# Rows instead of token blocks: a rotary projection whose halves change places by DMA

## The chip, the cores and the metric

The program runs on one core of a Trainium2 chip. A core has five engines that run their own instruction streams and wait for each other through semaphores: TensorE (PE: matmuls and transposes, results in PSUM), VectorE (DVE), ScalarE (ACT), GpSimd (POOL) and SyncE (SP), which here issues every DMA. The metric is the device time of one execution in microseconds: the median of three runs before is 1894.84 us (1893.67 to 1897.88).

## The reference

Two transformer blocks on 512 tokens of width 1024. The first has two layers. Each normalises x, projects it with one wide matrix, runs four attentions (a: latent, b: sliding window of 128 tokens, c: top-128 keys chosen by an indexer, d: with forget gates), four heads of 64 each, adds their projection to x, and then an MLP of width 4096. The second block has three dilated window attentions, a pooling branch and gates. What the change touches is the rotary embedding of b and c:

```
x1, x2 = xf[..., :half], xf[..., half:]
out = concatenate([x1 * cos - x2 * sin, x2 * cos + x1 * sin])
q_b = rope(b_q.reshape(B, S, H, Dh), pos)      # 4 heads of 64
k_b = rope(b_k.reshape(B, S, 2, Dh), pos)      # 2 heads of 64, each serves two query heads
q_c = rope(c_q.reshape(B, S, H, Dh), pos)
k_c = rope(c_k.reshape(B, S, H, Dh), pos)
```

## The kernel before

All arithmetic is float32. A matrix product is made of three matmuls in a reduced 32-bit format (`mm3`, lines 160 to 162): every operand is held as a high part and a low part, and high x high, high x low and low x high are added in PSUM. `split` (lines 167 and 168) makes such a pair: ScalarE writes the high part, VectorE subtracts it from the source and writes the low part.

Weights come in chunks of at most 128 x 1024 numbers. SP fetches them into two raw buffers (`send`, line 124); ScalarE makes the high half (line 143), VectorE or POOL the low half (line 144); four such pairs are kept, two chunks ahead of use. SP's queue is in order, so a fetch that waits for a buffer holds everything behind it.

The normalised input is kept as hT: 8 tiles of 128 features x 512 tokens. There are two ways to project. `token_proj` takes 128 tokens as the stationary operand and 256 weight columns as the moving one: 8 x 3 matmuls for each of four token blocks, result tokens x features. `feature_proj` takes 128 weight columns as the stationary operand and all 512 tokens as the moving one: result features x tokens, in one PSUM bank.

The attention scores need queries and keys as features x tokens ("seg", four planes of 128 features: two heads each). `roped` (line 586) projects by token blocks: for each block, VectorE multiplies by the cosines (line 286) and the exchanged halves by the signed sines (lines 287 and 288), POOL adds (line 289), TensorE turns the block with two 128x128 transposes (line 606), and `split` writes it into seg. It is called four times in each layer: queries and keys of b (line 750 and the one behind it; the keys' projection carries the values too) and queries and keys of c (lines 827 and 828). `lagged` puts a block's turn behind the next block's projection.

The order on each engine is made at build time: the program is written attention by attention (ORDER: latent inputs, indexer, scores and top-k for three token blocks, a, d's projections, d, c, b, and four output projections), and a scheduler lists the instructions of each engine by priority and by when it believes their inputs are there. So the projections of c and b fill TensorE while attention d runs, whose softmax and the top-k search (lines 581 and 582) keep VectorE. On the chip every engine then keeps its list strictly in order.

Two pools of scratch tiles matter: "tmp" (1024 columns, three buffers: norm rows, MLP activations and others) and "t2" (512 columns, four buffers: `half`, line 105). The constants are loaded at the start on SP's queue by `consts_first` (line 490), behind x and the first two weight chunks and ahead of the third and fourth.

Of the kernel before, what the change touches and what calls it, by code (L numbers as in the profile page):

```python
# [11 lines left out]
F32 = mybir.dt.float32  # L12
F32R = mybir.dt.float32r
AF = mybir.ActivationFunctionType
ALU = mybir.AluOpType
# [3 lines left out]
P = 128  # L19
S = 512  # L20
NB = S // P
D = 1024
KD = D // P
# [9 lines left out]
AHEAD, RAWS, HIS, TMPS, HALVES = 2, 2, 4, 3, 4  # L33
# [21 lines left out]
def halves(ap):  # L55
    return ap[:, :HALF], ap[:, HALF:]


class Kern:
# [43 lines left out]
        return self.tmp.tile([P, D], F32, tag="tmp", name=self.name("tmp"), bufs=TMPS)  # L103

    def half(self):
        return self.tmp.tile([P, S], F32, tag="t2", name=self.name("t2"), bufs=HALVES)

    def stat(self, cols=16):
        return self.small.tile([P, 16], F32, tag="st", name=self.name("st"), bufs=11)[:, :cols]
# [375 lines left out]
    def consts_first(self):  # L485
        nc, c, t = self.nc, self.fc, self.t

        def load(name, shape, src):
            o = c.tile(shape, F32, tag=name, name=name)
            nc.sync.dma_start(o, src)  # L490
            return o

        self.rope64 = load("rope64", [P, NB, 128], t["c_rope64"].rearrange("(b p) c -> p b c", p=P))
        self.rope32 = load("rope32", [P, NB, 64], t["c_rope32"].rearrange("(b p) c -> p b c", p=P))
        self.causal = load("causal", [P, S], t["c_causal"])
        self.swa = load("swa", [P, 256], t["c_swa"])
        self.tri = load("tri", [P, P], t["c_tri"])
        self.full_spans = [(0, (i + 1) * P, self.causal[:, S - (i + 1) * P :]) for i in range(NB)]
        self.ones = c.tile([P, P], F32, tag="ones", name="ones")
        nc.vector.memset(self.ones, 1.0)  # L500
# [85 lines left out]
    def roped(self, hT, ch, sg, at, take=None):  # L586


        nc = self.nc
        step = 2 if take else 1  # L590

        def rotate(b):
            pj = self.token_proj(hT, ch, b, 256)
            r = self.half()[:, :256]
            rv = r.rearrange("p (h c) -> p h c", c=64)
            n = 256 // step
            self.rope(rv[:, ::step], pj[:, :n].rearrange("p (h c) -> p h c", c=64), self.rope64, b)
            if take:
                nc.gpsimd.tensor_copy(rv[:, 1::2], rv[:, ::2])
                take(b, pj[:, n:256])  # L600
            return r

        def turn(b, r):
            pt = self.psum("tq")[:, :256]
            for c in range(2):
                nc.tensor.transpose(pt[:, c * P : (c + 1) * P], r[:, c * P : (c + 1) * P], self.ident)
            o = [t[:, at : at + 2, b * P : (b + 1) * P] for t in sg]
            self.split(o[0], o[1], pt.rearrange("p (m c) -> p m c", m=2))

        self.lagged(rotate, turn)  # L610

    def layer(self, l, hT, block):
        mixed = {}
# [125 lines left out]
    def window(self, l, hT):  # L739
        nc, t = self.nc, self.t  # L740
        sink = self.att.tile([P, 4], F32, tag="sink", name=self.name("sink"), bufs=1)
        nc.sync.dma_start(sink, t["swa_sinks"][l].partition_broadcast(P))
        sg = self.seg()
        vs = [self.new_v() for _ in range(2)]

        def values(b, src):
            for g in range(2):
                self.put_v(vs[g], b, src[:, g * 64 : g * 64 + 64].unsqueeze(1).to_broadcast([P, 2, 64]))

        self.roped(hT, self.weights(2), sg, 0)  # L750
        self.roped(hT, self.weights(2), sg, 2, values)
        spans = [(max(0, i - 1) * P, P if i == 0 else 2 * P, self.swa[:, 128:] if i == 0 else self.swa)
                 for i in range(NB)]
        return self.two_pairs(
            sg, vs, BAND, spans=spans, scale=0.125, sink=lambda h: sink[:, h : h + 1]
        )
# [67 lines left out]

    def selected(self, l, hT):
        sg = self.seg()
        self.roped(hT, self.weights(2), sg, 0)
        self.roped(hT, self.weights(2), sg, 2)
        ch = self.weights(2)
        vs = [self.new_v() for _ in range(2)]  # L830
        for b in range(NB):
            pj = self.token_proj(hT, ch, b, 256)
            for n in range(2):
                self.put_v(vs[n], b, pj[:, n * P : (n + 1) * P].rearrange("p (h c) -> p h c", c=64))
        return self.two_pairs(sg, vs, FULL, spans=[(0, n, a) for a, n in self.dsa], scale=0.125)
# [272 lines left out]
    def pair_inputs(self, hp, hT):  # L1108

        nc = self.nc  # L1110
# [10 lines left out]
        for g, which in HEADS2:  # L1121
# [12 lines left out]
            if which < 2:  # L1134
                o = self.new_qk()
                self.split(nat(o[:, 0]), nat(o[:, 1]), perm(pj), 0.125 if which == 0 else None)
                qk[g, which] = o
                continue
            vT = self.half()
            nc.scalar.copy(nat(vT), perm(pj))  # L1140
            v = self.new_v()
            pt = self.psum("tq")
# [299 lines left out]
    return np.ascontiguousarray(np.concatenate([c, c, -s, s], axis=1))  # L1442


def _bucket(n):
    exact = 16
    nf = np.maximum(n, 1).astype(np.float32)
    large = exact + (
        np.log(nf / np.float32(exact)) / np.float32(math.log(2048 / exact)) * np.float32(16)
    ).astype(np.int32)  # L1450
    return np.where(n < exact, n, np.minimum(large, 31))


def _constants():
# [14 lines left out]
    for g, w in enumerate((2, 4, 8, 16)):  # L1469
        short[g, :w] = np.float32(w) / np.arange(1, w + 1, dtype=np.float32)  # L1470
    return {
        "c_rope64": _rope_table(64), "c_rope32": _rope_table(32), "c_causal": causal, "c_swa": swa,
        "c_tri": tri, "c_buckets": buckets, "c_short": short,
    }

# [27 lines left out]
```

## Time and profile before

| | |
|---|---|
| median of three runs | 1894.84 us |
| the profiled execution | 1898.58 us |
| its span, first to last instruction | 1896.6 us |
| TensorE busy | 1816.0 us (96%) |
| VectorE busy | 1097.8 us (58%) |
| ScalarE busy | 876.0 us (46%) |
| POOL busy | 565.1 us (30%) |
| mean granted TensorE clock | 0.983 of full speed |

The profile is one execution. Matmuls are pipelined and their ends are modelled: one that is shown for 0.28 us can be followed by the next after 0.12 us. So what a matmul costs is read from the distance of starts in the timeline, not from its duration. A wait is put down to the engine that ended it.

### The profile page before, as it was taken

To read this page: it belongs to the slowest core of one execution; us is meant where nothing else is said; L and a number is where in the kernel's file an instruction comes from. 1 tells how busy PE (TensorE), PEld (TensorE's weight loads), DVE (VectorE), ACT (ScalarE), POOL (GpSimd) and SP (SyncE) were. 2 spreads that over 40 slices of the span, in tenths; PEclk is the share of its full clock that TensorE was granted. 3 is DMA by queue.
4 is the path that set the end of the run, shared out by engine and by line. 5 is a ranking of instruction groups with operands and counts; after the bars stand their busy time and mean duration, and the time that the engine had idled before them with its cause. 6 is when DMAs were issued, how large, how long until landed. Compare 5 with 4: busy or idle time off the path is not lost.

```text
span 1896.6 us, 25797 instructions
## 1 busy us (share of the span) xinstructions
PE 1816.0 (96%) x9414; PEld 1523.1 (80%) x9414; DVE 1097.8 (58%) x2437; ACT 876.0 (46%) x1882; POOL 565.1 (30%) x396
## 2 busy tenths in 40 slices
PE   7899998999999998999989999999799999998998
PEld 7788876888877887988778888888687888787886
DVE  6899667555554457997674433433726535446444
ACT  5666765233322346567762232332435444545443
POOL 1334331111111104334321111111146544433454
PEclk9999999999999999999999999999899999999999
DMA  4222112444456322322132333333332332322242
GB/s 162 59 75 71 46 49 81 118 149 145 145 150 179 106 56 66 81 59 73 45 99 68 98 103 100 95 95 100 101 101 60 112 91 79 90 62 62 83 150 100
DMA packets 220652, 178.52 MB, mean 94 GB/s; under 512 B 14734, under 2 KB 191278, under 8 KB 220526
## 3 DMA queue, kind: packets, MB, share of 16 engines
q1 hardware_dynamic: 220526, 176.88, 31.7%
q8 instruction: 74, 1.21, 0.3%
q14 instruction: 52, 0.43, 0.1%
HBM read 172.50 MB, written 8.03 MB: 95 GB/s over the span
## 4 chain that ended last, share of the span: by engine, by line
PE 80%; DVE 10%; DMA 4%; ACT 3%; issue 2%; SPq 0%; POOL 0%; ACTq 0%; DVEq 0%; POOLq 0%
PE acc L160 20%; PE acc L161 20%; PE acc L162 20%; PE sc L160 5%; PE sc L161 4%; PE sc L162 4%; DMA raw<-in_w_in_dram 2%; PE tp L385 2%; PE pv L311 1%; PE pv L310 1%; DVE dsa L582 1%; DVE dsa L561 1%; DVE m L581 1%; DMA raw<-in_w_down_dram 1%; DVE wlo L144 1%
## 5 line engine op out<-in xcount | busy, mean ns | idle before, releaser
L143 ACT ACTIVATE whi<-raw 128x1024 fp32r<-128x1024 f32 (+6 forms) x288 | 289.4, 1005 | 630.7 <-PE acc L161 274.0
L160 PE MATMUL acc<-hTh,whi 128*128 128x512 f32 (+1 forms) x1128 | 437.1, 389 | 12.4 <-DVE wd L1225 5.7
L161 PE MATMUL acc<-hTl,whi 128*128 128x512 f32 (+1 forms) x1128 | 434.2, 385 | 0.9 <-DVE hTl L168 0.9
L162 PE MATMUL acc<-hTh,wlo 128*128 128x512 f32 (+1 forms) x1128 | 432.9, 384 | 0.0
L144 POOL TENSOR_TENSOR wlo<-raw,whi 128x1024 fp32r<-128x1024 f32 (+4 forms) x143 | 312.1, 2187 | 353.5 <-ACT whi L143 331.5
L144 DVE TENSOR_TENSOR wlo<-raw,whi 128x1024 fp32r<-128x1024 f32 (+2 forms) x145 | 176.1, 1215 | 195.6 <-ACT whi L143 192.8
L876 POOL TENSOR_TENSOR tmp<-tmp 128x512 f32<-128x512 f32 x64 | 104.4, 1633 | 609.9 <-ACT tmp L874 609.9
L160 PEld LDWEIGHTS acc<-hTh,whi 128*128 128x128 f32 x1128 | 214.4, 191 | 56.9 <-ACT ms L1222 5.9
L161 PEld LDWEIGHTS acc<-hTl,whi 128*128 128x128 f32 x1128 | 214.6, 190 | 41.4 <-DVE hTl L168 2.4
L162 PEld LDWEIGHTS acc<-hTh,wlo 128*128 128x128 f32 x1128 | 214.3, 190 | 39.9
L160 PE MATMUL acc<-whi,hTh 128*128 128x256 f32 (+3 forms) x512 | 158.7, 312 | 6.4 <-DVE v L168 4.3
L162 PE MATMUL acc<-whi,hTl 128*128 128x256 f32 (+3 forms) x512 | 157.0, 307 | 0.2
L161 PE MATMUL acc<-wlo,hTh 128*128 128x256 f32 (+3 forms) x512 | 155.7, 305 | 0.4 <-DVE wlo L144 0.4
L160 PEld LDWEIGHTS acc<-whi,hTh 128*128 128x128 f32 x512 | 100.2, 196 | 12.0 <-DVE v L168 4.8
L162 PEld LDWEIGHTS acc<-whi,hTl 128*128 128x128 f32 x512 | 100.1, 195 | 3.3 <-DVE hTl L168 1.1
L161 PEld LDWEIGHTS acc<-wlo,hTh 128*128 128x128 f32 x512 | 100.3, 196 | 2.8 <-DVE wlo L144 0.8
L160 PE MATMUL acc<-whi,act 128*128 128x512 f32 x256 | 99.0, 392 | 3.5 <-DVE x L894 3.5
L161 PE MATMUL acc<-wlo,act 128*128 128x512 f32 x256 | 100.1, 391 | 0.0
L162 PE MATMUL sc<-whi,act 128*128 128x512 f32 x256 | 99.6, 389 | 0.0
L161 PE MATMUL sc<-wlo,act 128*128 128x512 f32 x256 | 99.6, 389 | 0.0
L160 PE MATMUL sc<-whi,act 128*128 128x512 f32 x256 | 99.6, 389 | 0.0
L162 PE MATMUL acc<-whi,act 128*128 128x512 f32 x256 | 98.8, 391 | 0.1
(341 smaller groups left out, 3475.9 us busy)
## 6 DMA issues: line engine op xcount, KB each, us to landing
raw<-in_w_in_dram SPq DMA_DIRECT2D x92, 512.0 KB, 4.0
raw<-in_w_up_dram SPq DMA_DIRECT2D x64, 512.0 KB, 4.2
raw<-in_w_down_dram SPq DMA_DIRECT2D x64, 512.0 KB, 3.3
raw<-in_w_out_dram SPq DMA_DIRECT2D x24, 512.0 KB, 3.5
raw<-in_w_ada_dram SPq DMA_DIRECT2D x24, 512.0 KB, 4.0
raw<-in_w_in_dram SPq DMA_DIRECT2D x8, 416.0 KB, 5.3
x<-in_x_dram SPq DMA_DIRECT2D x4, 512.0 KB
nrow<-neg SPq DMA_DIRECT2D x8, 256.0 KB
```

Of the source, the lines that this page charges most:

```text
L143: self.nc.scalar.activation(hi, raw, AF.Copy)
L144: self.lo_engine.tensor_tensor(lo, raw, f(hi), ALU.subtract)
L160: mm(out, lhsT[0], rhs[0], start=first, stop=False)
L161: mm(out, lhsT[0], rhs[1], start=False, stop=False)
L162: mm(out, lhsT[1], rhs[0], start=False, stop=last)
L310: mm(out, both, th[0], start=first, stop=False)
L311: mm(out[0:64], v[:, j, x, 0], th[1], start=False, stop=False)
L385: nc.tensor.transpose(pt[:, at : at + P], hd["p"][:, src : src + P], self.ident)
L561: nc.vector.scalar_tensor_tensor(a, e, r[:, 288 + h : 289 + h], self.causal[:, S - n :] if h == 0 else a, ALU.mult, ALU.add)
L581: nc.vector.max(out=m8, in_=a)
L582: nc.vector.match_replace(out=a, in_to_replace=m8, in_values=a, imm_value=TAKEN)
L876: nc.gpsimd.tensor_tensor(r[:, S:], r[:, :S], r[:, :S], ALU.mult)
```

## The change

A new method, `roped_rows`, replaces `roped` for the queries of b and for the queries and keys of c; the keys of b stay with `roped`. It projects 128 features over all 512 tokens at once (two halves m of 24 matmuls each), copies the result to SBUF on ScalarE, and lets four DMAs on SP's queue write each group of 32 partitions to its partner's place in a second tile. VectorE multiplies both tiles by rows of a new constant table (ropeT: cosines and signed sines as features x tokens), POOL adds them, and `split` writes seg; no transpose is needed. The scratch tile `a, t` is one "tmp" tile of two halves. To make room, "t2" tiles shrink from 512 to 384 columns, and the value copies of the second block move from "t2" to "tmp".

```diff
     def half(self):
-        return self.tmp.tile([P, S], F32, tag="t2", name=self.name("t2"), bufs=HALVES)
+        return self.tmp.tile([P, 384], F32, tag="t2", name=self.name("t2"), bufs=HALVES)
...
         self.rope32 = load("rope32", [P, NB, 64], t["c_rope32"].rearrange("(b p) c -> p b c", p=P))
+        self.ropeT = load("ropeT", [P, 2, S], t["c_ropeT"].rearrange("n p c -> p n c"))
...
+    def roped_rows(self, hT, chunks, sg, at):
+
+        nc = self.nc
+        for m in range(2):
+            out, cs, n = self.psum("acc"), slice(m * P, (m + 1) * P), 0
+            for c in chunks:
+                for k in range(c[0].shape[1]):
+                    self.mm3(
+                        out, (c[0][:, k, cs], c[1][:, k, cs]), (hT[0][:, n], hT[1][:, n]), n == 0, n == KD - 1
+                    )
+                    n += 1
+            a, t = halves(self.scratch())
+            nc.scalar.copy(a, out)
+            for q in range(4):
+
+                o = q ^ 1
+                nc.sync.dma_start(t[o * 32 : o * 32 + 32], a[q * 32 : q * 32 + 32])
+            nc.vector.tensor_tensor(a, a, self.ropeT[:, 0], ALU.mult)
+            nc.vector.tensor_tensor(t, t, self.ropeT[:, 1], ALU.mult)
+            nc.gpsimd.tensor_tensor(a, a, t, ALU.add)
+            self.split(sg[0][:, at + m], sg[1][:, at + m], a)
...
-        self.roped(hT, self.weights(2), sg, 0)
+        self.roped_rows(hT, self.weights(2), sg, 0)
         self.roped(hT, self.weights(2), sg, 2, values)
...
     def selected(self, l, hT):
         sg = self.seg()
-        self.roped(hT, self.weights(2), sg, 0)
-        self.roped(hT, self.weights(2), sg, 2)
+        self.roped_rows(hT, self.weights(2), sg, 0)
+        self.roped_rows(hT, self.weights(2), sg, 2)
...
-            vT = self.half()
+            vT = self.scratch()[:, :S]
```

TensorE, queries of attention c in the first layer, before: `acc_2203` is the third token block's result, `tq_2198` the turned first block, `tp_1463` a softmax tile of attention d.

```order
L162 MATMUL acc_2203<-whi_1736,hTl_111 128x256
L385 MATMUL tp_1463<-ident,p_1426 128x128
L606 MATMUL tq_2198<-ident,t_476_2161 128x128 x2
L160 MATMUL acc_2203<-whi_1736,hTh_110 128x256
L161 MATMUL acc_2203<-wlo_1737,hTh_110 128x256
L162 MATMUL acc_2203<-whi_1736,hTl_111 128x256
L385 MATMUL tp_1463<-ident,p_1426 128x128
```

The same engine and projection after the change: `acc_2138` ends the first half of the features, `acc_2174` begins the second, and `tp_1403` is again a softmax tile of d.

```order
L162 MATMUL acc_2138<-hTh_112,wlo_1772 128x512
L160 MATMUL acc_2174<-hTh_112,whi_1738 128x512
L161 MATMUL acc_2174<-hTl_113,whi_1738 128x512
L162 MATMUL acc_2174<-hTh_112,wlo_1739 128x512
L160 MATMUL acc_2174<-hTh_112,whi_1738 128x512
L161 MATMUL acc_2174<-hTl_113,whi_1738 128x512
L162 MATMUL acc_2174<-hTh_112,wlo_1739 128x512
L160 MATMUL acc_2174<-hTh_112,whi_1738 128x512
L160 MATMUL sc_1444<-seg_1236 128x384
L161 MATMUL sc_1444<-seg_1237,seg_1236 128x384
L162 MATMUL sc_1444<-seg_1236,seg_1237 128x384
```

The narrow matmuls and the two transposes are gone; scores and value products of d stand between the wide ones, and the transposes into `tp_1403` follow 16 rows behind the last row of `acc_2138`. On TensorE 8589 rows remain of 8910.

VectorE, the first rotation of the same projection, before:

```order
L168 TENSOR_TENSOR pt_1406<-tp_1401,pt_1406 128x512
L582 MATCH_REPLACE dsa_491<-m_204_915,dsa_491 128x512
L286 TENSOR_TENSOR t_476_2161<-acc_2136,rope_98 128x256
L287 TENSOR_TENSOR t_477_2162<-acc_2136,rope_98 128x4x32
L288 TENSOR_TENSOR t_477_2162<-acc_2136,rope_98 128x4x32
L359 RECIPROCAL sa_1430<-sa_1428 128x4
```

And after the change, where `tmp_2163` is the scratch tile that the four DMAs fill:

```order
L407 TENSOR_TENSOR total_1231<-pv_1200,total_1231 64x512
L349 TENSOR_SCALAR sa_1431<-sa_1429 128x4
L168 TENSOR_TENSOR pt_1408<-tp_1403,pt_1408 128x512
L630 TENSOR_TENSOR tmp_2163<-tmp_2163,ropeT 128x512
L631 TENSOR_TENSOR tmp_2163<-tmp_2163,ropeT 128x512
L583 MATCH_REPLACE dsa_493<-m_206_923,dsa_493 128x512
L582 MAX m_207_926<-dsa_493 128x8
```

The products read SBUF instead of PSUM, wait for DMAs instead of TensorE, and stand between a low part of d's probabilities and the top-k search. On SP's queue the four DMAs of a half stand behind two fetches of weights and ahead of the next.

## Rows read from the trace of the kernel before

**Rows 1.** The page, busy time, share of the span and instructions of each engine.
```profile
PE 1816.0 (96%) x9414; PEld 1523.1 (80%) x9414; DVE 1097.8 (58%) x2437; ACT 876.0 (46%) x1882; POOL 565.1 (30%) x396
```

**Rows 2.** Line 606 alone: duration ns min/median/max, first and last start, forms.
```profile
L606 PE MATMUL tq<-ident,t x64: 270/272/330, 153.4 to 925.4; 128*128 128x128 f32 x64
```

**Rows 3.** Windows: length, busy us (instructions) of PE, PEld, DVE, ACT, POOL; clock, DMA.
```profile
140.00:160.00 20.00, 18.86 (x122) 16.45 (x121) 19.31 (x59) 9.80 (x25) 3.86 (x5) 0.91 0.14 40
160.00:180.00 20.00, 20.00 (x151) 18.32 (x150) 16.96 (x63) 13.19 (x32) 11.27 (x10) 1.00 0.24 68
180.00:200.00 20.00, 19.80 (x139) 17.26 (x139) 18.10 (x60) 14.06 (x39) 6.19 (x4) 1.00 0.25 66
200.00:220.00 20.00, 20.00 (x147) 18.14 (x146) 10.73 (x37) 14.19 (x35) 8.79 (x6) 1.00 0.16 54
```

**Rows 4.** TensorE's waits, 135 to 205 and 205 to 320 us: total, times, longest.
```profile
PE sc L160 <- DVE sa L338: 1.5, 2, 1.1
...
PE acc L160 <- ACT mix L399: 1.5, 1, 1.5
```

**Rows 5.** Timeline of TensorE, 189 to 191 and 107 to 110 us: start, duration, line.
```profile
189.33 0.38 PE L606 MATMUL tq<-ident,t 128*128 128x128 f32 x2
189.46 0.36 PE L161 MATMUL acc<-wlo,hTh 128*128 128x256 f32 x1
189.66 0.28 PE L162 MATMUL acc<-whi,hTl 128*128 128x256 f32 x1
...
190.38 0.28 PE L162 MATMUL acc<-whi,hTl 128*128 128x256 f32 x1
...
107.20 0.39 PE L162 MATMUL acc<-hTh,wlo 128*128 128x512 f32 x1
...
109.93 0.39 PE L162 MATMUL acc<-hTh,wlo 128*128 128x512 f32 x1
```

**Rows 6.** Windows at the start; the last column is GB/s of the DMA engines.
```profile
5.00:10.00 5.00, 1.68 (x8) 1.57 (x8) 3.31 (x8) 3.27 (x9) 0.00 (x0) 1.00 1.01 375
15.00:20.00 5.00, 4.66 (x29) 3.75 (x27) 3.46 (x9) 3.01 (x7) 0.00 (x0) 1.00 0.51 179
```

**Rows 7.** Timeline of ScalarE: the third weight chunk's high half.
```profile
19.30 0.90 ACT L143 ACTIVATE whi<-raw 128x832 fp32r<-128x832 f32 x1 [1.42 <-DMA raw<-in_w_in_dram]
```

**Rows 8.** VectorE by line and form: busy us, mean ns | idle before it.
```profile
L168 DVE TENSOR_TENSOR seg<-tq,seg 128x256 fp32r<-128x256 f32 x32 | 13.3, 417 | 0.6 <-ACT seg L167 0.4
L286 DVE TENSOR_TENSOR t<-acc,rope 128x256 f32<-128x256 f32 x24 | 10.1, 419 | 7.4 <-PE acc L162 5.8 <-POOL mix L400 1.4 <-POOL wlo L144 0.3
L816 DVE TENSOR_TENSOR own<-nrow,causal 128x512 f32<-128x512 f32 x8 | 6.9, 866 | 2.6 <-DMA nrow<-neg 2.6
L288 DVE TENSOR_TENSOR t<-acc,rope 128x128 f32<-128x128 f32 x24 | 6.8, 282 | 0.0
```

**Rows 9.** The tile nrow: ns min/median/max of its reader on VectorE.
```profile
L816 DVE TENSOR_TENSOR own<-nrow,causal x8: 672/687/1718, 131.4 to 863.3; 128x512 f32<-128x512 f32 x8
```

**Rows 10.** Timeline of POOL and VectorE near 835 us.
```profile
833.99 2.40 POOL L144 TENSOR_TENSOR wlo<-raw,whi 128x1024 fp32r<-128x1024 f32 x1 [0.49 <-ACT whi L143]
...
835.22 1.72 DVE L816 TENSOR_TENSOR own<-nrow,causal 128x512 f32<-128x512 f32 x1
```

**Rows 11.** ScalarE and POOL by line and form.
```profile
L1140 ACT COPY t<-acc 128x512 f32<-128x512 f32 x12 | 6.9, 574 | 0.0
...
L876 POOL TENSOR_TENSOR tmp<-tmp 128x512 f32<-128x512 f32 x64 | 104.4, 1633 | 609.9 <-ACT tmp L874 609.9
```

**Rows 12.** Waits of SP's queue, 90 to 260 us: total, times, longest.
```profile
SPq L124 <- POOL wlo L144: 122.0, 17, 19.5
```

**Rows 13.** DMA issues: count, KB each, median us to landing.
```profile
b<-bt SPq DMA_DIRECT2D x16, 64.0 KB, 2.4
```

**Rows 14.** Timeline: a DMA's issue on SP and its reader on VectorE.
```profile
128.07 0.37 SPq L813 DMA_DIRECT2D nrow<-neg  x1
...
131.41 0.69 DVE L816 TENSOR_TENSOR own<-nrow,causal 128x512 f32<-128x512 f32 x1 [1.15 <-DMA nrow<-neg]
```

More of the change, by code (lines that the diff above doesn't have):

```diff
@@ L1442, in _rope_table, with _rope_rows @@
     return np.ascontiguousarray(np.concatenate([c, c, -s, s], axis=1))
+def _rope_rows():
+    t = _rope_table(64)
+    return np.ascontiguousarray(np.stack([np.concatenate([t[:, a : a + 64].T] * 2) for a in (0, 64)]))
 def _bucket(n):
@@ L1471, in _constants @@
     return {
-        "c_rope64": _rope_table(64), "c_rope32": _rope_table(32), "c_causal": causal, "c_swa": swa,
+        "c_rope64": _rope_table(64), "c_rope32": _rope_table(32), "c_ropeT": _rope_rows(), "c_causal": causal, "c_swa": swa,
         "c_tri": tri, "c_buckets": buckets, "c_short": short,
```

## The prediction

> **What bounds the kernel now.** I read the page first. TensorE is busy for 96% of the span, VectorE for 58% [rows 1]. A whole-span share says little about one stage, so I then looked for the stage of the change. The transposes of the roped blocks (line 606) show where it runs: 64 of them, from 153.4 to 925.4 us [rows 2], half in each layer. The projections before them begin near 140 us. The table by windows [rows 3] shows TensorE from 140 to 220 us at 18.9, 20.0, 19.8 and 20.0 of 20 us. VectorE is nearly as full up to 200 us (19.3, 17.0, 18.1), since it also runs the top-k search and two softmaxes, and falls to 10.7 of 20 afterwards. The waits of TensorE [rows 4] settle which is last: from 135 to 205 us its longest entry is 1.5 us, a score matmul behind a softmax; from 205 to 320 us it has a single wait of 1.5 us. I take the second layer, the same code, to be bound in the same way. So TensorE is the bound here, with VectorE close behind until 200 us. What shortens TensorE's stream should show at the end; what lengthens VectorE's shows only after about 5.6 us per layer, which is what it leaves idle from 140 to 200 us (0.69 + 3.04 + 1.90) [rows 3].
>
> **TensorE's part.** Three of four calls per layer change, six calls in all; the piece of the order on TensorE shows both forms.
> Transposes: each call loses 4 pairs, so 24 pairs go and 16 transposes (8 pairs, keys of the window) stay. One pair, at 189.33 us [rows 5]: the next matmul starts 0.13 us later, and the one behind that follows after 0.20 us where the six steps from 189.66 to 190.38 us take 0.12 each. A pair costs 0.13 + 0.08 = 0.21 us, so 24 x 0.21 = 5.0 us. Low end: 0.13 alone, where a switch of operand would stand there anyway, 3.1 us. High end: the median duration of one, 272 ns [rows 2], times 48, 13.1 us; these durations overlap the next start, so this is an outer bound.
> Matmuls: a call has 4 blocks x 24 matmuls of 256 columns; now 2 x 24 of 512. So 576 become 288 with the same columns. Two narrow ones take 2 x 0.12 = 0.24 us; a wide one takes 0.2275 us (12 steps in 2.73 us) [rows 5]. The gain is 288 x 0.0125 = 3.6 us. Low end: nothing, if two narrow equal one wide; a loss is excluded, since weight loads halve and the wide pitch is measured. High end: with the switch after the pair counted in (189.46 to 190.38 us, 7 steps, 0.131 each), 288 x 0.035 = 10.1 us.
> Together 8.6 us, ends 3.1 and 23.2; half of it in each layer.
>
> **The start.** A constant table of 512 KB (ropeT) enters SP's queue ahead of the causal mask, the vectors and the third and fourth weight chunk, all issued in order. There the DMA engines are full: 375 GB/s from 5 to 10 us [rows 6]. The third chunk's conversion starts at 19.30 us after waiting 1.42 us for its DMA [rows 7], and TensorE waits for that. 524,288 bytes at 375 GB/s are 1.4 us, which I take, once. Ends: nothing if the fetch slips in without delaying a chunk, 2.9 us at the 179 GB/s of 15 to 20 us [rows 6].
>
> **The other engines.** VectorE: a block cost 419 + 2 x 282 + 417 ns [rows 8] = 1.40 us; 24 blocks are 33.6 us. Now 12 halves have two products and one low part, 36 instructions of 128x512, all with both inputs in SBUF. The nearest row is "own" (line 816): same shape, both inputs in SBUF, same stretch, mean 866 ns [rows 8], from 672 to 1718 [rows 9]. That gives 36 x 0.866 = 31.2 us, 2.4 less; ends 36 x 0.672 = 24.2 (9.4 less) and 36 x 1.718 = 61.8 (28.2 more). Taken at nothing on the path, since TensorE is later.
> The spread has a visible cause: the 1.72 us instance at 835.22 us lies beside a POOL subtraction that runs from 833.99 us for 2.40 us [rows 10]. The Trainium skill, "SBUF — State Buffer", section "Who interferes with whom", says that a VectorE instruction with two SBUF inputs contends with a GpSimd instruction that reads SBUF, and one with a single SBUF input does not. The old products read PSUM, so by that rule they were immune and the new ones are not; the trace agrees for this instance. What it would do here is a rival below.
> ScalarE: 12 copies of 574 ns [rows 11] and 12 conversions of about that replace 24 smaller ones: under 13.8 us in all, on an engine with 6 to 10 us free in every 20 [rows 3]. POOL: 12 sums at 1633 ns [rows 11] are 19.6 us, on an engine in use for 19 to 56% [rows 3]. Both hidden; uncovered, each sum would add 1.6 us to a chain that has some 200 rows of TensorE work before its first reader (scores of the queries stand that far behind in the order).
> SP: 48 issues of 0.37 us [rows 14] are 8.9 us a layer. They stand behind a wait for a projection, with weight fetches and "nrow" (the forgetting attention's bias row) queued behind. SP has room: in 90 to 260 us it waited 122 us for POOL's halves before sending weights [rows 12], so a fetch behind a swap would mostly have waited anyway. Taken at nothing. If "nrow" slips, VectorE's "own" waits, at most a swap's length each time.
> Second part of the kernel: 12 value copies now take one of 3 large buffers instead of 4 small ones. Taken at nothing; if each waited for the transposes before it, about 12 x 0.574 us [rows 11] = 6.9 us.
>
> **The added wait.** VectorE's first product waits for four swaps. Path: copy 0.574, four issues of 0.37, landing 2.4 us (another 64 KB [rows 13]) to 3.3 us ("nrow", issued at 128.07, used at 131.41 us [rows 14]): 4.5 to 5.4 us after the last matmul. The order on VectorE puts a low part of a probability tile in front of it; the transposes that this needs stand 16 rows behind the last matmul of the projection, seven of them wide (7 x 0.2275 = 1.6 us). Covered by at least 1.6 us, so exposed by nothing to 3.8 us. I take nothing.
>
> **Sum.** 8.6 - 1.4 = 7.2 us less. The profiled execution took 1898.58 us (span 1896.6), 3.7 above the median of the runs, 1894.84. It becomes 1891.4; the median 1887.6, said as 1888.
>
> **Rivals.**
> More than that: the switches between operands go too. With 10.1 for the matmuls, 5.0 and -1.4: 13.7 less, 1881 us. For it: 0.20 us steps after every switch. Against: the wide stream is broken by other work as well. 0.12.
> No gain: two of the three calls per layer fall where VectorE is full, so TensorE only waits there instead. A third of 8.6 is 2.9, less 1.4: 1893.3. For it: 19.3 of 20 us on VectorE. Against: TensorE's waits there are under 2 us, and the order brings later projections forward as filling. 0.22.
> The port: VectorE's 36 instructions all stretch to 1.718 us beside POOL. 28.2 us more, 14.1 a layer; two thirds of it, 9.4, falls before 200 us, where 5.6 are free, so 3.8 a layer are exposed: -7.2 + 7.6, 1895.2 us. For it: the row at 835.22. Against: four of the eight "own" took no more than 687 ns, the median [rows 9], and POOL is idle for 44% or more [rows 3]. 0.12. The rule of the Trainium skill above, at its fullest, would come out here.
> Slower: VectorE stands in its queue for the swaps, 12 times, with the top-k rows and the softmax of the forgetting attention behind it and TensorE's value products behind those. It decides from (7.2 + 3.8) / 12 = 0.92 us each; at 1.2 us it is 14.4 - 7.2 = 7.2 slower, 1902 us. For it: landing times depend on 512 KB weight loads in the same queue. Against: the cover above, and 15% idle from 160 to 180 us. 0.14.
> That the change would not do what it says is excluded: the order has the wide matmuls and the swaps.
>
> **Chances.** Forecast 0.40 (its own range 1884 to 1892), others as given. A change under 0.2%, 3.8 us, cannot be told from none here. Faster: nearly all of the forecast (0.37), the larger gain (0.12) and the better tail of the two in the middle (0.06): 0.55. Same: 0.29. Slower: the swaps and a tail of the port: 0.16. The range 1880 to 1900 leaves out half of the larger gain and most of the slower case.
>
> **What would show it.** Line 606's successor with 16 transposes; wide matmuls at a pitch near 0.2275 us in the two stretches; TensorE still waiting under 2 us there; the third chunk's conversion near 20.7 us; the products' durations between 0.67 and 1.72 us; no wait of VectorE for a swap above 1 us. Wrong if VectorE shows waits for "tmp" DMAs, if TensorE's waits from 135 to 205 us grow by more than 4 us, or if a layer's stretch is not about 4 us shorter.

## The result

The changed kernel is slower: 1910.14 us (1905.42 to 1911.17) against 1894.78, ratio 1.0062, 95% interval 1.0046 to 1.0078. A second set of runs gave 1907.96 against 1896.78, 1.0064 (1.0050 to 1.0078). The forecast was 1888, the range 1880 to 1900. Medians and ratios below leave out two executions that took over 350 us longer than the others, one of e3 (2579.6 us) and one of the kernel before beside e5, e7, e8 and e9 (2256.43 us).

The page of the changed kernel, busy time and share of each engine:

```profile
PE 1814.4 (95%) x9078; PEld 1506.3 (79%) x9078; DVE 1108.2 (58%) x2377; ACT 879.6 (46%) x1882; POOL 567.6 (30%) x384
```

TensorE has 336 instructions fewer and the same busy time as in [rows 1], and the span is 12.7 us longer. A matmul at half the clock counts as busy for longer, so the busy share hides what happened. The windows that answer to [rows 3] (busy us of PE, PEld, DVE, ACT, POOL; clock; DMA) and the last one of the search in the second layer:

```profile
140.00:160.00 20.00, 20.00 (x99) 15.55 (x98) 19.70 (x53) 12.13 (x25) 8.20 (x5) 1.00 0.39 108
160.00:180.00 20.00, 17.59 (x105) 14.16 (x104) 19.90 (x53) 11.43 (x26) 10.85 (x6) 1.00 0.37 104
180.00:200.00 20.00, 18.52 (x113) 15.71 (x112) 17.56 (x50) 13.89 (x37) 7.47 (x4) 1.00 0.19 66
200.00:220.00 20.00, 20.00 (x121) 15.74 (x119) 14.06 (x37) 12.66 (x28) 9.71 (x7) 1.00 0.34 106
...
840.00:860.00 20.00, 16.53 (x97) 12.85 (x95) 19.87 (x46) 10.99 (x25) 9.82 (x6) 1.00 0.35 97
```

VectorE is fuller than before from 140 to 180 us (39.6 of 40 us, was 36.3), and TensorE is not full there any more: 17.59 of 20 where it had 20.00. TensorE's waits in the changed kernel, 135 to 205 us (the stretch of the first row of [rows 4]) and, behind the "...", 800 to 900 us of the second layer:

```profile
PE sc L160 <- DVE sa L338: 3.3, 2, 2.0
PE pv L310 <- DVE total L407: 0.4, 1, 0.4
PE acc L160 <- DVE v L168: 0.2, 1, 0.2
...
PE sc L160 <- DVE sa L338: 5.3, 5, 1.6
PE pv L310 <- DVE total L407: 1.3, 1, 1.3
PE pv L311 <- DVE pt L168: 0.5, 1, 0.5
```

The waiting instruction is a score matmul of attention d: its bank of PSUM is free only when VectorE has read the scores before it (line 338). What keeps VectorE stands in its timeline before two of those waits (TensorE's score matmuls at 851.15 and 860.32 us waited 1.63 and 1.62 us):

```profile
846.29 2.89 DVE L630 TENSOR_TENSOR tmp<-tmp,ropeT 128x512 f32<-128x512 f32 x1
849.11 0.68 DVE L631 TENSOR_TENSOR tmp<-tmp,ropeT 128x512 f32<-128x512 f32 x1
...
849.78 0.67 DVE L583 MATCH_REPLACE8 dsa<-m,dsa 128x512 f32<-128x512 f32 x1
850.38 0.28 DVE L338 CUSTOM_DVE_ANT_0 p<-sc,own 128x128 f32<-128x128 f32 x1
...
858.12 0.67 DVE L583 MATCH_REPLACE8 dsa<-m,dsa 128x512 f32<-128x512 f32 x1
858.72 0.68 DVE L630 TENSOR_TENSOR tmp<-tmp,ropeT 128x512 f32<-128x512 f32 x1
859.31 0.68 DVE L631 TENSOR_TENSOR tmp<-tmp,ropeT 128x512 f32<-128x512 f32 x1
...
860.00 0.25 DVE L338 CUSTOM_DVE_ANT_0 p<-sc,own 128x128 f32<-128x128 f32 x1
```

Both times the two products of a rotated half, and a step of the search, stand directly ahead of the softmax row (line 338) that TensorE waits for. There is no swap in that wait. But the first product took 2.89 us where its neighbour took 0.68: these 2.2 us more are longer than the 1.63 us that TensorE then waited. The longest wait of this kind, 2.03 us for the score matmul at 171.4 us, also stands behind a stretched instruction, "own" (line 839), which took 0.67 us at its shortest; from its end to the softmax row VectorE ran without a gap. The second row is the POOL subtraction beside the product of 846.29:

```profile
165.74 3.49 DVE L839 TENSOR_TENSOR own<-nrow,causal 128x512 f32<-128x512 f32 x1
...
845.83 2.81 POOL L144 TENSOR_TENSOR wlo<-raw,whi 128x1024 fp32r<-128x1024 f32 x1 [2.49 <-ACT whi L143]
```

Then the clock: windows of 5 us of the changed kernel, same columns.

```profile
850.00:855.00 5.00, 3.85 (x28) 3.54 (x29) 4.94 (x17) 1.32 (x3) 3.48 (x2) 1.00 0.58 182
855.00:860.00 5.00, 3.16 (x23) 2.68 (x22) 5.00 (x10) 3.42 (x12) 1.30 (x1) 1.00 0.48 129
860.00:865.00 5.00, 4.68 (x15) 3.28 (x16) 4.85 (x24) 3.34 (x8) 1.28 (x1) 0.57 0.00 0
865.00:870.00 5.00, 5.00 (x23) 4.45 (x22) 3.99 (x10) 1.72 (x4) 1.28 (x1) 0.50 0.18 52
870.00:875.00 5.00, 5.00 (x38) 4.88 (x38) 0.63 (x2) 1.75 (x5) 0.34 (x1) 0.91 0.00 0
```

After two windows in which TensorE was busy for 3.85 and 3.16 of 5 us, the granted clock is 0.57, 0.50 and 0.91: for some 10 us the lower level, 1.2 GHz, though TensorE has work again (5.00 of 5). (1 - clock) x 5 us over these windows is 5.1 us lost. Before, TensorE was busy throughout this place and the clock stayed at its upper level:

```profile
855.00:860.00 5.00, 5.00 (x35) 4.06 (x34) 4.70 (x17) 1.87 (x4) 3.21 (x3) 1.00 0.38 108
860.00:865.00 5.00, 5.00 (x37) 4.39 (x36) 4.71 (x12) 3.16 (x8) 1.27 (x1) 1.00 0.50 155
```

The Trainium skill, "TensorE: Matmul & The Clock Gate", Part 1, says that a gate halves TensorE's clock when the engine has been little busy; the rows above agree, the fall stands behind waits. Not every fall does: in the kernel before with half of the search (e7, below) TensorE had no wait in the 15 us ahead of this one, and counts as busy throughout.

```profile
115.00:120.00 5.00, 5.00 (x22) 4.08 (x22) 3.49 (x11) 3.55 (x10) 0.12 (x1) 0.66 0.04 11
```

The other rows that answer: line 607 is the successor of 606 [rows 2]; two starts, 22 steps apart, of wide matmuls [rows 5]; the third weight chunk [rows 7]; VectorE's instructions by form, 100 to 1010 us [rows 8, 9]; the issue of the swaps [rows 13]; two products that waited for a swap.

```profile
L607 PE MATMUL tq<-ident,t x16: 270/272/328, 219.4 to 924.8; 128*128 128x128 f32 x16
```

```profile
192.68 0.40 PE L161 MATMUL acc<-hTl,whi 128*128 128x512 f32 x1
...
197.72 0.39 PE L162 MATMUL acc<-hTh,wlo 128*128 128x512 f32 x1
```

```profile
20.02 0.89 ACT L143 ACTIVATE whi<-raw 128x832 fp32r<-128x832 f32 x1
```

```profile
L630 DVE TENSOR_TENSOR tmp<-tmp,ropeT 128x512 f32<-128x512 f32 x12 | 12.6, 1051 | 9.8 <-DMA tmp<-tmp 9.4 <-issue 0.4
L168 DVE TENSOR_TENSOR seg<-tmp,seg 128x512 fp32r<-128x512 f32 x12 | 11.3, 945 | 1.1 <-ACT seg L167 1.1
L631 DVE TENSOR_TENSOR tmp<-tmp,ropeT 128x512 f32<-128x512 f32 x12 | 9.4, 779 | 0.0
```

```profile
L839 DVE TENSOR_TENSOR own<-nrow,causal 128x512 f32<-128x512 f32 x8 | 10.9, 1357 | 4.4 <-DMA nrow<-neg 4.4
```

```profile
tmp<-tmp SPq DMA_DIRECT2D x48, 64.0 KB, 2.0
```

```profile
830.31 0.69 DVE L630 TENSOR_TENSOR tmp<-tmp,ropeT 128x512 f32<-128x512 f32 x1 [1.71 <-DMA tmp<-tmp]
...
892.14 1.77 DVE L630 TENSOR_TENSOR tmp<-tmp,ropeT 128x512 f32<-128x512 f32 x1 [4.43 <-DMA tmp<-tmp]
```

### The profile page after: what moved, and what is told of

The parts are those of the page before. It is cut to its first block, busy times and chain, and to the rows that moved or that the text cites. A ratio compares the mean times of both kernels' runs of the same rounds, so it can differ in the third digit from the quotient of the medians.

```text
span 1909.3 us, 25121 instructions
## 1 busy us (share of the span) xinstructions
PE 1814.4 (95%) x9078; PEld 1506.3 (79%) x9078; DVE 1108.2 (58%) x2377; ACT 879.6 (46%) x1882; POOL 567.6 (30%) x384
## 4 chain that ended last, share of the span: by engine, by line
PE 74%; DVE 13%; DMA 5%; ACT 4%; issue 2%; POOL 1%; SPq 0%; DVEq 0%; ACTq 0%; POOLq 0%
PE acc L160 19%; PE acc L161 19%; PE acc L162 18%; PE sc L160 4%; PE sc L161 4%; PE sc L162 4%; DMA raw<-in_w_in_dram 2%; DVE m L582 1%; DVE dsa L583 1%; PE tp L385 1%; DVE wlo L144 1%; DMA raw<-in_w_ada_dram 1%; ACT whi L143 1%; PE pv L311 1%; PE pv L310 1%
## 5 line engine op out<-in xcount | busy, mean ns | idle before, releaser
L160 PE MATMUL acc<-hTh,whi 128*128 128x512 f32 (+1 forms) x1224 | 476.9, 391 | 13.5 <-DVE wd L1248 5.7
L161 PE MATMUL acc<-hTl,whi 128*128 128x512 f32 (+1 forms) x1224 | 473.3, 387 | 0.9 <-DVE hTl L168 0.8
L162 PE MATMUL acc<-hTh,wlo 128*128 128x512 f32 (+1 forms) x1224 | 471.8, 386 | 0.0
L162 PEld LDWEIGHTS acc<-hTh,wlo 128*128 128x128 f32 x1224 | 232.9, 190 | 44.4 <-issue 0.7
L160 PE MATMUL acc<-whi,hTh 128*128 128x256 f32 (+3 forms) x320 | 100.9, 317 | 7.5 <-DVE v L168 4.5
L162 PE MATMUL acc<-whi,hTl 128*128 128x256 f32 (+3 forms) x320 | 99.7, 312 | 0.2
L161 PE MATMUL acc<-wlo,hTh 128*128 128x256 f32 (+3 forms) x320 | 99.1, 311 | 0.4 <-DVE wlo L144 0.4
L917 DVE TENSOR_TENSOR x<-acc,x 128x512 f32<-128x512 f32 x64 | 43.8, 687 | 68.9 <-PE acc L162 68.9
L400 POOL TENSOR_TENSOR mix<-total,mix 64x512 fp32r<-64x512 f32 x32 | 44.5, 1392 | 131.2 <-ACT mix L399 129.2
L167 ACT ACTIVATE pt<-tp 128x512 fp32r<-128x512 f32 (+3 forms) x128 | 62.3, 513 | 41.0 <-PE tp L385 21.0
```

What stands on the lines that cost most here:

```text
L160: mm(out, lhsT[0], rhs[0], start=first, stop=False)
L161: mm(out, lhsT[0], rhs[1], start=False, stop=False)
L162: mm(out, lhsT[1], rhs[0], start=False, stop=last)
L167: self.nc.scalar.activation(hi, src, AF.Copy)
L400: nc.gpsimd.tensor_tensor(lo, o, f(hi), ALU.subtract)
L917: nc.vector.tensor_tensor(xs, out, xs, ALU.add)
```

## The experiments

Three theories. W: VectorE's queue is held by the wait for the swaps, and SP's by their issue. V: while the top-k search runs, VectorE is full; TensorE's saving turns into waits there, and the clock falls behind them. O: the loss is in the order of TensorE's list, which puts d's scores ahead of projection rows that could run.

For each profile the table adds up the two attention stretches (from the first step of the search to where TensorE first waits for the norm ahead of the MLP: in the kernel before 71.4 to 315.4 and 745.5 to 987.6 us), TensorE's waits from 100 and 780 us to those ends, and the clock lost there ((1 - granted) x length over windows of 5 us). A wait at the lower clock counts in both, so waits plus clock is an upper bound.

| kernel | median, and before on the same chip, us | ratio (95%) | two stretches | waits | clock |
|---|---|---|---|---|---|
| before | 1894.84 | | 486.1 | 6.6 | 1.7 |
| changed | 1910.14, 1894.78 | 1.0062 (1.0046-1.0078) | 497.0 | 18.4 | 11.9 |
| changed again (e12) | 1907.96, 1896.78 | 1.0064 (1.0050-1.0078) | 498.2 | 16.3 | 13.6 |
| e1 scratch tiles only | 1895.09, 1893.62 | 1.0011 (0.9997-1.0025) | 486.1 | 6.4 | 1.7 |
| e2 rows for b only | 1894.20, 1893.62 | 1.0007 (0.9996-1.0018) | 482.5 | 7.1 | 0.0 |
| e3 rows for c only | 1905.77, 1893.62 | 1.0069 (1.0047-1.0092) | 495.7 | 13.2 | 10.2 |
| e4 no swaps | 1901.11, 1893.62 | 1.0048 (1.0033-1.0064) | 491.1 | 16.3 | 8.6 |
| e5 exchange by ScalarE | 1904.03, 1895.75 | 1.0054 (1.0033-1.0076) | 494.7 | 17.6 | 6.8 |
| e6 swaps on ScalarE's queue | 1903.60, 1896.78 | 1.0038 (1.0024-1.0051) | 489.2 | 11.4 | 13.7 |
| e7 before, half search | 1892.75, 1895.75 | 0.9984 (0.9969-0.9999) | 485.6 | 3.4 | 5.1 |
| e8 changed, half search | 1882.65, 1895.75 | 0.9942 (0.9923-0.9960) | 475.1 | 3.2 | 1.7 |
| e9 second product on POOL | 1905.35, 1895.75 | 1.0055 (1.0036-1.0075) | 493.5 | 19.1 | - |
| e10 changed, b ahead of c | 1913.39, 1896.78 | 1.0096 (1.0074-1.0118) | 501.1 | 20.7 | 15.3 |
| e11 before, b ahead of c | 1904.50, 1896.78 | 1.0042 (1.0028-1.0057) | 496.2 | 14.4 | 5.1 |
| e13 changed, d later | 1922.12, 1892.66 | 1.0155 (1.0138-1.0172) | 510.4 | 20.6 | 30.7 |
| e14 before, d later | 1901.70, 1892.66 | 1.0045 (1.0030-1.0060) | 495.3 | 15.0 | 3.4 |
| e15 changed, d later still | 1920.91, 1892.66 | 1.0152 (1.0137-1.0168) | 512.3 | 23.5 | 32.5 |
| e16 d later, ScalarE's queue | 1922.04, 1892.66 | 1.0155 (1.0138-1.0173) | 515.0 | 22.4 | 25.6 |
| e17 b only, ScalarE's queue | 1896.24, 1894.52 | 1.0011 (0.9999-1.0023) | 488.9 | 9.1 | 5.1 |
| e18 VectorE relieved | 1897.28, 1894.52 | 1.0021 (1.0008-1.0033) | 493.1 | 14.1 | 12.0 |

(e9's profile shows TensorE's full speed as 0.95, so its clock isn't compared.)

In the profiles of the changed kernel most of the loss lies in the second layer, though the code is the same: the first stretch takes 244.4 us (244.0 before) and the second 252.6 (242.1); in e12 it is 246.5 and 251.7. Waits and lost clock together rise by 5.1 us in the first and by 16.9 in the second.

**Where the loss is: parts alone.** e1 takes the kernel before with the scratch tiles of the change:

```
-        return self.tmp.tile([P, S], F32, tag="t2", ...
+        return self.tmp.tile([P, 384], F32, tag="t2", ...
-            vT = self.half()
+            vT = self.scratch()[:, :S]
```

> The kernel before with only the two changes of scratch: t2 tiles of 384 columns, and the value copies of the second block in a tmp buffer; all projections by token blocks. In the changed kernel the second block (1382 to 1851 us) came out about 3 us later than it began (9.8 to 12.8). Theory 'the scratch tiles do that': 1897 to 1898 us here, the 3 us between 1640 and 1820. Theory 'the second block only varies with the order or from run to run': within 1 us of the kernel before, 1894 to 1896.

e2 and e3 take the changed kernel with `roped` back in c and in b:

```
 e2, selected():
-        self.roped_rows(hT, self.weights(2), sg, 0)
-        self.roped_rows(hT, self.weights(2), sg, 2)
+        self.roped(hT, self.weights(2), sg, 0)
+        self.roped(hT, self.weights(2), sg, 2)
 e3, window():
-        self.roped_rows(hT, self.weights(2), sg, 0)
+        self.roped(hT, self.weights(2), sg, 0)
```

> The change with rows for the queries of b alone (2 calls); c by token blocks as before. B's projection runs after the top-k search, where VectorE has slack and TensorE is the bound. Theory W (VectorE held by the swaps) and theory V (a full VectorE before 200 us can't take the gain, and TensorE then waits and loses clock) both say the gain shows here: a third of 8.6 is 2.9 less, 1892, or up to 1895 if the scratch tiles cost 3. Theory 'the swap waits count wherever they are' (3.3 and 4.4 us in front of b's products in the changed kernel): 1898 to 1900.

> The change with rows for the queries and keys of c alone (4 calls); b by token blocks as before. Theories W and V: the whole loss is here, 1905 to 1912 us, with TensorE waiting for softmax rows 8 to 10 us in 780 to 1010 us and a fall of the granted clock behind it. If b's swaps are what costs: 1890 to 1894.

The scratch tiles cost nothing that can be measured. c alone gives the whole loss (1.0069); b alone is level. b's rows come when the search is over; c's rows fall into it. W and V both put a gain of 2.9 us (a ratio of 0.9985) into e2; its interval, 0.9996 to 1.0018, leaves that out. In the profile of e2, one execution, the two stretches are 3.6 us shorter; the medians don't show it.

**The swaps.** e4 leaves the exchange out:

```
-            for q in range(4):
-                o = q ^ 1
-                nc.sync.dma_start(t[o * 32 : o * 32 + 32], a[q * 32 : q * 32 + 32])
-            nc.vector.tensor_tensor(a, a, self.ropeT[:, 0], ALU.mult)
-            nc.vector.tensor_tensor(t, t, self.ropeT[:, 1], ALU.mult)
+            nc.vector.tensor_tensor(t, a, self.ropeT[:, 1], ALU.mult)
+            nc.vector.tensor_tensor(a, a, self.ropeT[:, 0], ALU.mult)
```

> The changed kernel without the 48 swaps: the second product takes the same tile as the first (the exchange of the halves is left out), all other instructions are there. Theory W (the wait for the swaps, and their place in SP's queue): the loss goes and the gain of TensorE shows, 1887 to 1893 us. Theory V (VectorE is full, whatever it waits for): 1903 to 1909, TensorE's waits for softmax rows stay at 4 us or more in each layer and the clock still falls behind them.

e5 lets ScalarE exchange the halves, and the first product reads PSUM; e6 only issues the swaps elsewhere:

```
 e5:
-            nc.scalar.copy(a, out)
...
-                nc.sync.dma_start(t[o * 32 : o * 32 + 32], a[q * 32 : q * 32 + 32])
-            nc.vector.tensor_tensor(a, a, self.ropeT[:, 0], ALU.mult)
+                nc.scalar.copy(t[o * 32 : o * 32 + 32], out[q * 32 : q * 32 + 32])
+            nc.vector.tensor_tensor(a, out, self.ropeT[:, 0], ALU.mult)
 e6:
-                nc.sync.dma_start(t[o * 32 ...
+                nc.scalar.dma_start(t[o * 32 ...
```

> The changed kernel with the exchange done by ScalarE: four copies of 32x512 from PSUM into the partner's partitions take the place of one copy and four DMAs, and the first product reads PSUM. No DMA wait, no place in SP's queue, one of two products with a single SBUF input; VectorE's count is unchanged, ScalarE gets about 4 x 0.5 us per half instead of 0.57. Theory W (swaps) and the port theory (two SBUF inputs beside POOL): 1886 to 1893. Theory V (VectorE full): 1898 to 1906, as without the swaps (1901).

> The changed kernel with the 48 swaps issued on ScalarE's queue, right behind the copy, instead of SP's, where they stood behind weight fetches. Theory W: the first products wait less and 4 to 8 us come back, 1899 to 1905. Theory V: within 3 us of the changed kernel; ScalarE's issues (about 0.4 us each, 1.6 per half) may cost as much as they bring.

> The changed kernel itself, for a closer ratio on the same chip as the next three: 1.0062 before, interval 1.0046 to 1.0078; without the swaps it was 1.0048 (1.0033 to 1.0064). Theory W needs the swaps to be most of the loss, a ratio of 1.008 or more here; theory V says 1.005 to 1.007, so that the swaps were a third of it or less.

Without swaps 7.5 us of the loss remain (2 us under V's range, 8 over W's), so W is not its main part. The swaps' place in SP's queue may be a part: 4.4 us came back in e6 (1907.96 to 1903.60, same chip), as W had said and V had not, the intervals of the ratios just touching. But no swaps at all (1.0048) are no better than swaps on ScalarE's queue (1.0038), and that queue brought nothing in e16 and e17 below. So its price isn't settled. The ratio of e12, 1.0064, is in V's range (1.005 to 1.007) and under W's 1.008. TensorE's waits for softmax rows without any swap (e4, 785 to 970 us):

```profile
PE sc L160 <- DVE sa L338: 2.6, 4, 1.0
PE pv L310 <- DVE total L407: 1.1, 1, 1.1
PE tp L385 <- DVE pt L168: 0.6, 1, 0.6
```

In e5 no DMA is waited for, and no product is stretched (by form, 100 to 1010 us):

```profile
L628 DVE TENSOR_TENSOR tmp<-acc,ropeT 128x512 f32<-128x512 f32 x12 | 8.2, 686 | 5.3 <-ACT tmp L627 5.1
L629 DVE TENSOR_TENSOR tmp<-tmp,ropeT 128x512 f32<-128x512 f32 x12 | 8.2, 681 | 0.0
```

The products took 22.0 us in the changed kernel and 16.4 here, and the run is still 8 us slower than before. So POOL beside the products alone isn't the main part. It isn't excluded as a part: e5 also gives ScalarE 27.7 us of copies in place of 6.9, and leaves "own" and the low parts of seg with two inputs in SBUF, and two of these low parts took 2.8 us.

**VectorE's load.** e7 and e8 leave half of the search out of both kernels:

```
-        for _ in range(TOPK // 8):
+        for _ in range(TOPK // 16):
```

> The kernel before with half of the top-k search left out (8 steps instead of 16 for each of three token blocks), some 25 us less of VectorE in each layer, just where it is full. TensorE was the bound with waits of 2 to 4 us a layer, so little moves: 1884 to 1894. It is the base for the next run.

> The changed kernel with the same half of the search left out. Theory V: with VectorE no longer full TensorE's saving shows, and this run comes out 4 to 9 us below the kernel before with half the search; TensorE's waits for softmax rows go, and no fall of the clock is left inside the attention. Theory 'TensorE's own order or the table is the cost': it stays 8 to 13 us above.

The change is now a gain: 1882.65 against 1892.75, 10.1 us by the medians, 0.0042 or 8.0 us by the ratios, whose intervals don't meet. The edit does more than halve the load beside c's rows: the last step of the search starts at 124.2 and 793.2 us in e7, at 123.0 and 788.6 in e8, ahead of c's projections, and the scheduler orders every engine's list anew. VectorE has room in e8, and TensorE is full:

```profile
820.00:840.00 20.00, 20.00 (x101) 14.96 (x100) 13.52 (x39) 14.81 (x35) 9.69 (x6) 1.00 0.38 105
840.00:860.00 20.00, 19.97 (x141) 17.57 (x141) 14.26 (x46) 14.83 (x38) 7.70 (x6) 1.00 0.19 54
```

e9 and e18 take work off VectorE and give it to POOL:

```
 e9 and e18:
-            nc.vector.tensor_tensor(t, t, self.ropeT[:, 1], ALU.mult)
+            nc.gpsimd.tensor_tensor(t, t, self.ropeT[:, 1], ALU.mult)
 e18 also (and the swaps as in e6):
-            self.split(sg[0][:, at + m], sg[1][:, at + m], a)
+            nc.scalar.activation(sg[0][:, at + m], a, AF.Copy)
+            nc.gpsimd.tensor_tensor(sg[1][:, at + m], a, f(sg[0][:, at + m]), ALU.subtract)
```

> The changed kernel with the second product (signed sines) on POOL instead of VectorE: 6 x 0.68 = 4.1 us less of VectorE in each layer, 6 x 1.3 us more of POOL, which is idle for half of the time. The swaps and the wait for them by the first product stay. Theory V: a part of the loss comes back, 1897 to 1904. Theory W: nothing comes back, 1905 to 1912. If POOL's load on the shared port is what counts: 1910 or more.

> The changed kernel with the second product and the low part of each half on POOL and the swaps on ScalarE's queue: 12 x 0.68 = 8.2 us less of VectorE in each layer, 12 x 1.3 us more of POOL. Theory V with VectorE's load as the measure: TensorE's waits and the falls of the clock shrink, 1888 to 1898. If it isn't VectorE's amount of work but that the search fills it until it ends, whatever else is taken off: the search only ends earlier and the time stays at 1900 to 1907.

4.1 us less a layer (e9) brought nothing that can be told from the changed kernel: a miss of V's expectation, and what W had said. Of e9's 19.1 us of waits 9.5 are two single ones for a softmax row, at 183.5 and 854.2 us. 8.2 us less and the other queue (e18) brought two thirds of the loss back, 1.0064 to 1.0021, as V had said. How it did so its profile doesn't show: waits and lost clock are hardly smaller than in the changed kernel, and a single wait for a softmax row is now 4.6 us (785 to 970 us):

```profile
PE sc L160 <- DVE sa L338: 5.5, 2, 4.6
PE pv L311 <- DVE pt L168: 2.0, 1, 2.0
```

e10 and e11 write b ahead of c, so that the search might spread:

```
-ORDER = "LI123AZVPDCBadcb"
+ORDER = "LI123AZVPDBCadbc"
```

> The changed kernel with attention b ahead of c in the written order (projections stay C, then B; the attentions go a, d, b, c instead of a, d, c, b), so that the top-k search, which only c needs, may spread over more of the layer. Theory V: VectorE is no longer full while the rows of c and b are projected, and this run comes out 4 to 9 us below the same order with the kernel before. If VectorE's load isn't the cause: 8 to 13 us above it.

> The kernel before with attention b ahead of c: the base for the run with the change. TensorE was the bound, so the time hardly moves: 1885 to 1900.

The search didn't spread: its last step starts at 184.9 and 866.7 us, where the changed kernel had 186.0 and 865.1. And the edit moves all of b, its projections too, ahead of c, though the expectation says that they stay: in e10 VectorE's products for b's queries (149 to 160 and 832 to 843 us) now fall into the search, and those for c (199 to 232 and 882 to 914 us) come behind it. Two of the products in the first layer, b's and c's first:

```profile
159.84 0.69 DVE L630 TENSOR_TENSOR tmp<-tmp,ropeT 128x512 f32<-128x512 f32 x1
...
198.64 2.64 DVE L630 TENSOR_TENSOR tmp<-tmp,ropeT 128x512 f32<-128x512 f32 x1 [3.20 <-DMA tmp<-tmp]
```

So one call of rows a layer instead of two meets the search, and the change still costs as much (8.9 us against e11, which is itself 7.7 us slower than the kernel before, beyond its expectation). V as put ahead of the run is missed: the loss is not tied to c's rows, and it doesn't go with the number of rows beside the search.

**The order of TensorE's list.** e13, e14 and e15 move d's work behind in the scheduler's priority, by 600 (e15: 2000); e16 adds e6's queue:

```
+                at = self.tc.cur_priority
+                self.tc.cur_priority = at + 600
                 mixed["d"] = self.forgetting()
+                self.tc.cur_priority -= 600
```

> The changed kernel with attention d 600 places later in priority, so that the list of TensorE has more of c's and b's projection rows ahead of each of d's scores (about 11, 11 and 14 us of them instead of 5 to 8 us in the middle of the projections). Theory O (the order of TensorE's list): the waits for softmax rows get smaller and the time falls to 1888 to 1900. Theory V (VectorE has no time left): the waits come later, 1904 to 1912.

> The kernel before with attention d 600 places later in priority: the base for the run before. Its waits were 2 to 4 us a layer, so there is little to win; d's chain may end later, 1892 to 1902.

> The changed kernel with attention d 2000 places later. The rows of the first two calls are as in the run with 600; behind them still more projection rows come first. Theory O: as with 600 or a few us lower or higher, since later stages have fewer rows left to fill in, 1886 to 1902. Theory V: 1904 to 1915.

> The changed kernel with attention d 600 places later and the swaps on ScalarE's queue. The swaps' queue alone gave 4 us (1903.6 against 1908.0). If the two parts add: 3 to 5 us below the run with d later alone. If the list with more rows in between hides the swaps anyway: the same as that run.

O's expectation failed: more rows between the scores made it slower still, 1.0155 against 1.0064, some 17 us by the ratios; V's ranges, up to 1912 and 1915, were missed too. The kernel before is 9 us slower in this order (e14), so the change costs 20 here. ScalarE's queue brought nothing (e16 against e13). The waits are about as long (20.6), but they come together, and the clock lost is 30.7 us instead of 12 to 14. Windows of e13:

```profile
900.00:905.00 5.00, 5.00 (x18) 3.45 (x17) 3.89 (x10) 4.98 (x15) 1.27 (x1) 0.50 0.00 0
905.00:910.00 5.00, 5.00 (x19) 3.80 (x17) 2.85 (x12) 2.85 (x8) 0.00 (x0) 0.50 0.01 3
910.00:915.00 5.00, 4.71 (x16) 3.32 (x16) 2.42 (x5) 4.98 (x16) 1.27 (x1) 0.50 0.00 0
915.00:920.00 5.00, 5.00 (x17) 3.47 (x16) 2.12 (x9) 1.22 (x4) 0.00 (x0) 0.50 0.00 0
920.00:925.00 5.00, 4.61 (x17) 3.76 (x16) 2.83 (x12) 4.95 (x16) 0.00 (x0) 0.50 0.00 0
```

TensorE counts as busy for nearly all of these 25 us, with 16 to 19 matmuls in 5 us, at half the clock. Its timeline there holds scores, transposes and value products alone: the projection rows, put first, end at 893 us, and the next ones stand at 926. Another order may still be better; this one wasn't.

**No version beats both.** e17 was tried for it:

> Rows for the queries of b alone, with their swaps on ScalarE's queue. A third of 8.6, 2.9 us, is what TensorE saves; with SP's queue the run was level with the kernel before (ratio 1.0007). If the swaps' place in SP's queue ate the saving: 2 to 3 us below the kernel before, ratio 0.9985. If the saving is lost in waits elsewhere: 1.000 to 1.001.

It is level with the kernel before, or 1 to 2 us slower.

## Why the prediction was wrong

**TensorE's part: right, and not where it counts.** 16 transposes are left. The wide pitch is 5.04 us / 22 = 0.229 instead of 0.2275, so the matmuls give 288 x (0.240 - 0.229) = 3.2 rather than 3.6, and the sum is 8.2 rather than 8.6. e8 against e7 shows 8 to 10 us where VectorE is not full; in their profiles the stretches are 10.5 us shorter, 3.6 of it smaller waits and less lost clock, so that some 7 are left for TensorE's own work.

**The step that failed: "Taken at nothing on the path, since TensorE is later".** The durations of the 36 instructions were fair (33.3 us; 31.2 were expected), but VectorE's busy time rose by 10.4 us where 2.4 less were expected, 4.0 of it in "own" (6.9 to 10.9). And TensorE and VectorE were nearly level until the search ends, 193 and 871 us, and two of the three calls fall there. Where TensorE's list reaches d's scores, VectorE's has two products or a low part, 0.68 us each or longer, ahead of the softmax row. TensorE's waits went from 6.6 to 18.4 us. "TensorE's waits there are under 2 us" was read as room; with both engines nearly full it was none. The second layer, taken to be bound like the first, has most of the loss; the sign that the prediction named, waits from 135 to 205 us that grow by more than 4 us, lies in the first and did not come (1.9 to 3.9).

**The rival "no gain" had the place right and the price wrong.** It let TensorE wait for as long as it had saved, and no longer. The waits are longer than the saving, and behind them the clock falls, which no term held: 1.7 us lost before, 11.9 after. Saving 8.6 at the forecast's size, waits 11.8 and clock 10.2: 13.4 more as the upper bound; the stretches are 10.9 longer, the span 12.7.

**The added wait: "I take nothing" was wrong, but small.** The swaps of three of the twelve halves were late for VectorE, 3.3, 1.7 and 4.4 us, not one in each half of 1.2. The 3.3 and the 4.4 stand where the search is over (204.9 and 892.1 us). The rival "slower" named the side rightly and the mechanism for the smaller part: without swaps, 7.5 us of loss stay.

**SP: "Taken at nothing" was too little, perhaps.** An issue of a swap took 0.58 us in the median, not 0.37, and another queue brought 4.4 us (e6), but nothing in e16 and e17.

**The port.** The Trainium skill, "SBUF — State Buffer", "Who interferes with whom", says that a VectorE instruction with two SBUF inputs contends with a GpSimd instruction that reads SBUF. The trace agrees: the product at 846.29 took 2.89 us beside a POOL subtraction from 845.83 for 2.81 us, and "own" went from 866 to 1357 ns in the mean. With the products' stretching gone (e5) the loss was 8.3 us, and with it (23.2 us of products in e8, 22.0 in the changed kernel) half the search left a gain, so it isn't the cause by itself. But two of the three longest waits for a softmax row stand behind an instruction so stretched, and no run takes this away alone: as a part of the cause the rival is open.

**The start: mis-sized.** The third chunk came 0.7 us later (20.02), not 1.4, and the first step of the search came at 70.95 instead of 71.36 us: nothing of it was left.

**Second part of the kernel: as taken.** e1 is level.

Shown: in the order of the two kernels rows for c bring the whole loss and rows for b none (e3, e2), and with half of the search the change is a gain (e8, e7). Likely, but with intervals that overlap or touch: the swaps and their queue are a quarter to two fifths (e4, e6). Argued from rows only: that products ahead of softmax rows are what lengthens the waits, and that in e8 it is VectorE's room, not the other order of the lists, that gives the gain. Open: why e9 brought nothing and e18 much, why one call beside the search costs as much as two (e10), and how the loss divides between VectorE's load, the stretching beside POOL and the order of the two lists, since each edit also changed the order.

## What to carry to other kernels

Where two engines are level in a stage, time taken off one can come back as its wait for the other, as here; count it as gain only in the part where the other one has room, and see what new work stands in the other's queue ahead of the results that are waited for. Put the clock into the sum: here waits of 1.63, 0.54 and 1.62 us within 10 us cost 5.1 us more in the 10 us behind them. To test whether an engine off the path hides a gain, halve its largest job in both kernels and compare the pair; but where a scheduler makes the order, look at how far the lists changed with it, since the pair can't tell load from order.

## What had not been expected of the hardware

In e13 TensorE stayed at 0.50 of its clock from 900 to 925 us, where its waits were 0.7 us in all and its busy share was 92% and more in each 5 us; only scores, transposes and value products ran there. And a ScalarE copy of 32 partitions x 512 took 577 ns (48 of them in e5, second row), as long as one of 128 x 512 (573 ns in the changed kernel, first row), so an exchange of the halves in four copies cost four full copies.

```profile
L625 ACT COPY tmp<-acc 128x512 f32<-128x512 f32 x12 | 6.9, 573 | 1.0 <-PE acc L162 1.0
...
L627 ACT COPY tmp<-acc 32x512 f32<-32x512 f32 x48 | 27.7, 577 | 10.3 <-PE acc L162 9.6
```
